# Places of split weights by the order of products, a last group's sums and a head's rotation moved from GpSimd to VectorE, and two spreadings sharing a pair of banks, in a fp32 hybrid layer step on one Trainium2 core

## The chip, the cores and the metric

The kernel runs on one core of a Trainium2 chip (trn2). The metric is the device time of one execution in microseconds; the median of three runs of the kernel before is 2238.82 us (2236.67 to 2243.57). A core has a matrix engine (TensorE, PE in the profile; PEld is its loading of weights), VectorE (DVE), ScalarE (ACT), GpSimd (POOL), SyncE (SP), whose queue issues most of the DMAs here, an on-chip memory of 128 partitions (SBUF), and accumulator banks of 128 partitions by 2 KB (PSUM), into which matmuls write.

## What is computed

One step of a layer: 1024 prompt frames and 64 sample frames, D_MODEL 1024, all in float32.

```python
xn = RMSNorm(x); q, k, v, gates, ... = split(xn @ w_in)
A = retention(q, k, v)          # 4 heads of 256, chunks of 64, rotary on q and k
B = sliding_window_attention()  # 16 heads of 64, 2 K/V heads
x += (sigmoid(ga) * A + sigmoid(gb) * B) @ w_mix_out
x += CrossAttn(RMSNorm(x), memory)
x += SwiGLU(RMSNorm(x))         # w_gate, w_up: 1024 -> 2816, w_down back
y = RMSNorm(x)
```

with, for the rotary part, `concat([x1 * cos - x2 * sin, x2 * cos + x1 * sin])`. The outputs are y for both streams, the retention states and the attention caches.

## The kernel before

**Precision.** Each float32 operand is split into two parts, `hi` (a cast by ScalarE, line 123) and `lo` (the rest, a subtraction by VectorE, line 124), and each product is three matmuls: weight hi by x hi (L209), weight hi by x lo (L210), weight lo by x hi (L212). Frames stand along the free dimension: T = 1088, in two halves of HALF = 544, each of two spans of HC = 272 columns. So nearly every matmul of the kernel is 128 rows by 128 columns of weights by 272 columns of x.

**Strassen.** Dense layers run as 2 x 2 block products by Strassen's scheme: seven products (`strassen`, L250) instead of eight. x stands as operands B11, B21, B22 and the combinations T1 to T4; the combinations of the weights are made anew for each group by `weight_ops` (L171): four sums and differences by GpSimd in the buffers `raw` (L187, L188, L190, L193), and a split of each result into a buffer named `wq` by `put`. The weights are *made* in the order P1, P2, P7, P6, P5, P3, P4, and the products *run* in the order P1, P2, P6, P5, P7, P3, P4. There are two buffers `raw` for the two loaded weight pieces of a group, so the next group's pieces load when the last split of this one is done. A product accumulates in a pair of PSUM banks (`bank_pair`, name `pq`); in the FFN there are four pairs. VectorE adds products and running sums (u1, u2, u3, u5; L256), and `emit` consumes the results.

`new_op` (L144) gives the buffer of a split weight: five places in a ring; once a phase late in the projections has made room, a sixth place, which is given to every sixth weight made. The first group of a phase goes without Strassen (`plain`, L229), since its operand combinations aren't there yet: eight products of half the depth.

**What sets the order.** The code is run through a scheduler that simulates a timeline and decides the order of the instructions on each engine, from priorities, data and free buffers. On the chip each engine takes its own queue in that order, and a semaphore holds it up where what it needs isn't there. `issue_after(x)` orders later instructions behind x in the schedule. `later` is a list of functions that are called at a point inside the next product (`run_later`).

**The four places that matter here.**

1. *First head.* The phase begins with the keys, values and queries of head 0; `rotated` (L600) takes two halves a and b of 128 rows: four VectorE products with cos and sin (L610 to L613), then a -= sb and b += sa on GpSimd (L614, L615), then stores of a and b to DRAM (`d_qkv`). They come back as `ks`, `qs`, are split, and the retention starts with `pss` (scores, L153). The same function rotates the other heads later, when the retention of an earlier head is under way; the products of a coming head then fill TensorE's gaps between the steps of the retention's chain (scores `pss`, output `po`, the spreading of norms `pb`, L843).
2. *The norm ahead of the FFN.* `rstd_f`, the reciprocal root for each frame, is computed as a column of values per block of 128 frames and spread over 128 partitions by matmuls with the identity into a bank, and copied out by ScalarE (`spread`, L327 to L335). Three columns of frames are spread: the last two inside the first FFN group (`plain` of w_gate), by `run_later` ahead of the seventh of its eight block products. In the same stretch the operand combinations T2, T3, T4 are made (VectorE sums `xg`, L1352, ScalarE casts, L123) by `other_sums`.
3. *w_down.* The hidden rows of the FFN are handled in three groups (GROUPS), each with four pairs of output blocks (m = 0, 2, 4, 6). `down.add` (L1514) adds a result to the output tiles y: a product in PSUM by VectorE (L1517), a running sum in SBUF by GpSimd (L1519). y is eight tiles, one of which lies in rstd_f. In the last group (`part=True` in `strassen`), P2 and P4 are left to the finish, which does them by thirds of the columns, so each m has five products.
4. *The last group's tail.* `complete` squares the finished half (L1527, L1530) and sums the squares (L1531) for the final norm.

Of the kernel before, what the change touches and what calls it, by code (L numbers as in the profile page):

```python
# [14 lines left out]
ALU = mybir.AluOpType  # L15
# [94 lines left out]
class Kernel:  # L110
# [32 lines left out]

    def new_op(self):  # L144

        self.turns += self.sixth is not None
        if self.turns and self.turns % 6 == 0:
            return self.sixth.tile([P, 2, 512], F32R, tag="wq", bufs=1, name="wq")
        return self.wp.tile([P, 2, 512], F32R, tag="wq", bufs=5, name="wq")

# [19 lines left out]
    def weight_ops(self, raws, n=512, skip=()):  # L170

        nc = self.nc
        half = [[raws[i][:, j * n:(j + 1) * n] for j in range(2)] for i in range(2)]
        (a11, a12), (a21, a22) = half
        add, sub = ALU.add, ALU.subtract
        w = {}

        def put(name, src):
            if name in skip:
                return  # L180
            q = w[name] = self.new_op()
            self.split(src, q[:, 0, :n], q[:, 1, :n])

        tt = nc.gpsimd.tensor_tensor
        put("P1", a11)
        put("P2", a12)
        tt(out=a11, in0=a11, in1=a21, op=sub)  # L187
        tt(out=a21, in0=a21, in1=a22, op=add)  # L188
        put("P7", a11)
        tt(out=a11, in0=a22, in1=a11, op=sub)  # L190
        put("P6", a11)
        put("P5", a21)
        tt(out=a12, in0=a12, in1=a11, op=sub)  # L193
        put("P3", a12)
        put("P4", a22)
        return w
# [54 lines left out]
    def strassen(self, w, x, emit, part=False):  # L251


        nc = self.nc
        u1, u2, u3, u5 = (self.fp.tile([P, 2, HC], F32, tag=t, bufs=1, name=t) for t in ("u1", "u2", "u3", "u5"))
        add = lambda out, a, b: nc.vector.tensor_tensor(out=out, in0=a, in1=b, op=ALU.add)  # L256
        ps = self.product(w, x, "P1", "B11")
        self.run_later()
        nc.scalar.copy(u1, ps)
        emit(0, 0, None if part else self.product(w, x, "P2", "B21"), u1)  # L260
        add(u2, self.product(w, x, "P6", "T2"), u1)
        add(u5, self.product(w, x, "P5", "T1"), u2)
        ps = self.product(w, x, "P7", "T3")
        add(u3, ps, u2)
        emit(1, 1, ps, u5)
        emit(0, 1, self.product(w, x, "P3", "B22"), u5)
        emit(1, 0, None if part else self.product(w, x, "P4", "T4"), u3)
# [59 lines left out]
    def spread(self, out, r):  # L327
# [7 lines left out]
        nc.scalar.copy(out, pb[:, :n])  # L335

    def run(self):
        nc, tc, io = self.nc, self.tc, self.io
        with ExitStack() as ctx:
# [34 lines left out]
            with ExitStack() as sctx:  # L374
# [3 lines left out]
                self.left = sctx.enter_context(ExitStack())  # L378
                self.sixth, self.turns = None, 0
                self.wp = self.left.enter_context(tc.tile_pool(name="weights", bufs=2, reuse_waits="tile"))  # L380
# [172 lines left out]
    def project_phase(self):  # L553
        nc, tc, io = self.nc, self.tc, self.io
        with ExitStack() as ctx:
# [42 lines left out]
            def rotated(w, h, j):  # L598
# [3 lines left out]
                def emit(i, t, ps, sb):  # L602
# [10 lines left out]
                    tt(out=b, in0=b, in1=cos, op=ALU.mult)  # L613
                    nc.gpsimd.tensor_tensor(out=a, in0=a, in1=sb, op=ALU.subtract)  # L614
                    nc.gpsimd.tensor_tensor(out=b, in0=b, in1=sa, op=ALU.add)  # L615
                    self.store(self.d_qkv[j, 2 * h, :, half(t)], a)
# [50 lines left out]
            for idx, w, act in ((1, "w_ga", AF.Sigmoid), (0, "w_rg", AF.Silu), (2, "w_gb", AF.Sigmoid)):  # L667
                for m in range(0, KT, 2):
                    if (idx, m) == (1, 6):
                        fctx.close()  # L670
                        self.sixth = self.left.enter_context(tc.tile_pool(name="sixth", bufs=1, reuse_waits="tile"))
                        self.sums_pool(ctx)
                        op = ctx.enter_context(tc.tile_pool(name="op", bufs=1, reuse_waits="tile"))
                        mp = ctx.enter_context(tc.tile_pool(name="mp", bufs=1, reuse_waits="tile"))
                        self.dense_psum = lambda: self.norm_psum("pd")
                        memory = self.memory_phase(mp)
# [617 lines left out]
    def cross_out_phase(self):  # L1294
        nc, tc, io = self.nc, self.tc, self.io
        with ExitStack() as ctx:
# [9 lines left out]
            for m, u, (c0, n) in self.m_major(units, CH, tail=2):  # L1306
# [12 lines left out]
                if m == KT - 1:  # L1319
# [5 lines left out]
                    if len(norms) < 3:  # L1325
                        self.later += norms[-1][:3 - len(norms)]
            self.later, self.last_roots = [norms[1][1], norms[2][1]], norms[2][0]

# [41 lines left out]
    def operands_late(self, sums=None):  # L1370
# [6 lines left out]
        if sums is not None:  # L1377
            sums()
            self.other_sums()

    def other_sums(self):
        qs = [self.quarters(k) for k in range(4)]
        for k, (b11, b12, b21, b22) in enumerate(qs):
            self.put_sum("T2", k, b12, b22, b12)
        for k, (b11, b12, b21, b22) in enumerate(qs):
# [19 lines left out]
    def gate_up(self, pairs):  # L1405
# [5 lines left out]
        def roots_then_sums():  # L1411
            self.last_roots()
            with self.tc.issue_after(self.last_step):
                self.other_sums()

# [91 lines left out]
    def down(self, starts):  # L1507
# [5 lines left out]
        half = lambda m, t: y[m][:, t * HALF:(t + 1) * HALF]  # L1513
        def add(m, i, t, ps, sb):  # L1514
            v = half(m + i, t).rearrange("p (b c) -> p b c", b=2)
            if ps is not None:
                nc.vector.tensor_tensor(out=v, in0=ps, in1=v, op=ALU.add)  # L1517
            if sb is not None:
                nc.gpsimd.tensor_tensor(out=v, in0=sb, in1=v, op=ALU.add)  # L1519

# [15 lines left out]
        for gi, g in enumerate(GROUPS):  # L1536
            last = gi == len(GROUPS) - 1
            f0, n = starts[gi], g * P // 2
            for m in range(0, KT, 2):
                def emit(i, t, ps, sb, m=m):  # L1540
                    add(m, i, t, ps, sb)
                    if last and t == 1:
# [218 lines left out]
```

## Time and profile before

| | |
|---|---|
| three runs, median (lowest to highest) | 2238.82 us (2236.67 to 2243.57) |
| the profiled execution's own time | 2245.45 us |
| its span in the trace | 2243.6 us |
| mean granted TensorE clock | 0.988 |
| instructions | 41715 |
| ScalarE busy | 885.9 us (39%) |
| PEld busy | 2107.2 us (94%) |
| DMA packets | 181958, 290.85 MB |

The profile is of one execution. In its rows an instruction is shown as start, duration (both us), engine, line, operation, output <- inputs with buffer numbers left out, shape and count; a bracket at the end gives the idle time of the engine just before and what ended it. A view by windows gives for each stretch the busy time of every engine (with the number of instructions in parentheses), then the granted TensorE clock as a share of full speed, the share of the DMA engines, and GB/s. The page's view in slices gives a digit for each fortieth of the span (56 us).

### The profile page before, as it was taken

The numbers are of one execution on the slowest core, as the hardware profiler recorded it, in microseconds if no ns is written. First come the engines' busy times: TensorE is split into PE (matmuls) and PEld (weight loads), VectorE is DVE, ScalarE is ACT, GpSimd is POOL, SyncE is SP. The second block draws the span as 40 slices with busy tenths as digits, with TensorE's granted clock in tenths as the row PEclk, the third lists the DMA queues.
The fourth block names the chain that finished last, engine by engine and source line by source line (L and its number), as shares of the span: only waits on it lengthen the run. The fifth ranks groups of instructions, "written<-read, shape, count | busy, mean of one in ns | idle before, by whom it ended". The sixth has DMA issues, their size and how long they took to land.

```text
span 2243.6 us, 41715 instructions
## 1 busy us (share of the span) xinstructions
PE 2171.3 (97%) x16435; PEld 2107.2 (94%) x16435; DVE 1592.7 (71%) x2622; ACT 885.9 (39%) x1898; POOL 706.0 (31%) x474
## 2 busy tenths in 40 slices
PE   8899999999999999999999999999999999999986
PEld 8899999999999987779999999999999999999985
DVE  8986878676677668765455565777777777877587
ACT  7333333435434346553233343333223223434333
POOL 1441533342253122220000000015556565434462
PEclk9999999999999999999999999999999999999998
DMA  5433345443544475327343111513342332475323
GB/s 198 160 109 111 118 124 133 136 126 114 166 142 166 157 245 185 108 71 217 118 153 119 39 50 55 164 63 98 117 147 88 103 122 89 164 258 177 93 77 108
DMA packets 181958, 290.85 MB, mean 130 GB/s; under 512 B 40290, under 2 KB 110338, under 8 KB 181762
## 3 DMA queue, kind: packets, MB, share of 16 engines
q1 hardware_dynamic: 177218, 278.74, 39.1%
q10 hardware_dynamic: 4032, 7.80, 0.9%
q8 instruction: 130, 2.13, 0.4%
q0 software_dynamic: 512, 1.64, 0.2%
q14 instruction: 66, 0.54, 0.1%
HBM read 196.95 MB, written 91.16 MB: 128 GB/s over the span
## 4 chain that ended last, share of the span: by engine, by line
PE 72%; DVE 13%; DMA 5%; issue 3%; POOL 3%; ACT 3%; SPq 0%; DVEq 0%; POOLq 0%; ACTq 0%
PE pq L212 13%; PE pq L209 13%; PE pq L210 13%; PE pd L153 7%; PE pd L155 7%; PE pd L154 7%; DVE wq L124 3%; PE pout L1004 1%; DMA hl<-d_op 1%; DVE B L124 1%; PE pss L944 1%; DMA raw<-w_up 1%; DVE T L124 1%; POOL raw L190 1%; ACT wq L123 1%
## 5 line engine op out<-in xcount | busy, mean ns | idle before, releaser
L124 DVE TENSOR_TENSOR wq<-raw,wq 128x512 fp32r<-128x512 f32 (+1 forms) x499 | 461.6, 929 | 152.7 <-ACT wq L123 150.4
L123 ACT CAST wq<-raw 128x512 fp32r<-128x512 f32 (+1 forms) x499 | 303.3, 613 | 560.8 <-PE pq L212 226.5
L209 PE MATMUL pq<-T,wq 128*128 128x272 f32 x1832 | 493.5, 289 | 17.9 <-ACT wq L123 8.7
L210 PE MATMUL pq<-T,wq 128*128 128x272 f32 x1832 | 493.4, 289 | 0.0
L210 PE MATMUL pq<-B,wq 128*128 128x272 f32 x1592 | 430.2, 290 | 7.9 <-DVE B L124 7.9
L209 PE MATMUL pq<-B,wq 128*128 128x272 f32 x1592 | 427.7, 289 | 0.2 <-ACT B L123 0.2
L212 PE MATMUL pq<-T,wq 128*128 128x272 f32 x1832 | 383.2, 290 | 0.0
L209 PEld LDWEIGHTS pq<-T,wq 128*128 128x128 f32 x1832 | 346.4, 189 | 19.9 <-ACT wq L123 9.4
L187 POOL TENSOR_TENSOR raw<-raw 128x512 f32<-128x512 f32 (+1 forms) x59 | 78.2, 1326 | 908.0 <-DVE rs_r L295 483.8
L210 PEld LDWEIGHTS pq<-T,wq 128*128 128x128 f32 x1832 | 346.4, 189 | 0.0
L212 PE MATMUL pq<-B,wq 128*128 128x272 f32 x1592 | 333.9, 290 | 0.0
L210 PEld LDWEIGHTS pq<-B,wq 128*128 128x128 f32 x1592 | 301.1, 189 | 9.8 <-DVE B L124 9.4
L209 PEld LDWEIGHTS pq<-B,wq 128*128 128x128 f32 x1592 | 300.9, 189 | 0.8 <-issue 0.4
L212 PEld LDWEIGHTS pq<-T,wq 128*128 128x128 f32 x1832 | 291.0, 190 | 1.1 <-issue 1.1
L212 PEld LDWEIGHTS pq<-B,wq 128*128 128x128 f32 x1592 | 253.4, 190 | 0.5 <-issue 0.3
L256 DVE TENSOR_TENSOR u<-pq,u 128x544 f32<-128x544 f32 x177 | 127.2, 720 | 88.7 <-PE pq L212 87.7
L190 POOL TENSOR_TENSOR raw<-raw 128x512 f32<-128x512 f32 (+1 forms) x59 | 87.7, 1486 | 131.3 <-DVE wq L124 128.8
L579 DVE TENSOR_TENSOR stage<-pq,u 128x544 f32<-128x544 f32 x112 | 80.4, 718 | 27.1 <-PE pq L212 25.1
L193 POOL TENSOR_TENSOR raw<-raw 128x512 f32<-128x512 f32 (+1 forms) x59 | 86.9, 1474 | 16.6 <-DVE wq L124 13.0
L971 POOL TENSOR_TENSOR t<-t,den 128x768 f32<-128x768 f32 (+2 forms) x34 | 48.9, 1439 | 132.5 <-DVE den L969 33.2
L188 POOL TENSOR_TENSOR raw<-raw 128x512 f32<-128x512 f32 (+1 forms) x59 | 88.5, 1500 | 3.6
L1519 POOL TENSOR_TENSOR y<-u,y 128x544 f32<-128x544 f32 x38 | 64.9, 1711 | 75.3 <-DVE y L1517 58.3
(382 smaller groups left out, 4671.2 us busy)
## 6 DMA issues: line engine op xcount, KB each, us to landing
hl<-d_op SPq DMA_DIRECT2D x85, 272.0 KB, 4.5
d_qkv<-stage SPq DMA_DIRECT2D x44, 272.0 KB, 2.4
d_op<-stage SPq DMA_DIRECT2D x44, 272.0 KB, 2.3
d_op<-ht SPq DMA_DIRECT2D x44, 272.0 KB, 3.3
raw<-w_gate SPq DMA_DIRECT2D x22, 512.0 KB, 3.5
raw<-w_up SPq DMA_DIRECT2D x22, 512.0 KB, 3.7
raw<-w_down SPq DMA_DIRECT2D x16, 512.0 KB, 4.4
d_gate<-stage ACTq DMA_DIRECT2D x28, 272.0 KB, 2.6
```

The source lines that it names most:

```text
L123: self.last_cast = self.nc.scalar.copy(hi, src).ins
L124: return self.nc.vector.tensor_tensor(out=lo, in0=src, in1=hi.bitcast(F32), op=ALU.subtract).ins
L153: mm(ps, wh, xh, start=start, stop=False)
L154: mm(ps, wh, xl, start=False, stop=False)
L155: self.last_mm = mm(ps, wl, xh, start=False, stop=stop).ins
L188: tt(out=a21, in0=a21, in1=a22, op=add)
L190: tt(out=a11, in0=a22, in1=a11, op=sub)
L193: tt(out=a12, in0=a12, in1=a11, op=sub)
L209: mm(ps[:, c, :HC], w[:, 0, ks], x[:, 0, cs], start=start, stop=False)
L210: mm(ps[:, c, :HC], w[:, 0, ks], x[:, 1, cs], start=False, stop=False)
L212: self.last_mm = mm(ps[:, c, :HC], w[:, 1, ks], x[:, 0, c * HC:(c + 1) * HC], start=False, stop=stop).ins
L256: add = lambda out, a, b: nc.vector.tensor_tensor(out=out, in0=a, in1=b, op=ALU.add)
```

## The change

Five edits, in one diff (the names are those above):

- `new_op` no longer gives the sixth place to every sixth weight but to the one for which the sixth place's last holder is used earlier than those of the five (the list `held`), counting uses in the order of products: `put` passes the number of turns by which P7, P6 and P5 run later or earlier than they are made.
- `strassen(part=True)`, of the last group of w_down: the first product is added to y straight from PSUM (VectorE) instead of from its copy u1 (GpSimd).
- `down.add`: in the last group the running sums in SBUF are added by VectorE too.
- `rotated`: for head 0 the last subtraction and addition are VectorE's.
- `spread_both`: the last two spreadings of rstd_f go into the two banks of one pair, with both copies behind them; T3 and T4 (`last_sums`) are issued behind the copies, and only T2 (`second_sums`) ahead.

```diff
-    def new_op(self):
-        self.turns += self.sixth is not None
-        if self.turns and self.turns % 6 == 0:
+    def new_op(self, ahead=0):
+        self.turns += 1
+        turn = self.turns + ahead
+        if self.sixth is not None and self.last_held < min(self.held):
+            self.last_held = turn
             return self.sixth.tile([P, 2, 512], F32R, tag="wq", bufs=1, name="wq")
+        self.held = sorted(self.held)[-4:] + [turn]
         return self.wp.tile([P, 2, 512], F32R, tag="wq", bufs=5, name="wq")
...
-            q = w[name] = self.new_op()
+            q = w[name] = self.new_op({"P7": 2, "P6": -1, "P5": -1}.get(name, 0))
...
         ps = self.product(w, x, "P1", "B11")
         self.run_later()
         nc.scalar.copy(u1, ps)
-        emit(0, 0, None if part else self.product(w, x, "P2", "B21"), u1)
+        if part:
+            emit(0, 0, ps, None)
+        else:
+            emit(0, 0, self.product(w, x, "P2", "B21"), u1)
...
+    def spread_both(self, outs, rs):
+        pb = self.bank_pair()
+        for i, (out, r) in enumerate(zip(outs, rs)):
+            for j, (a, w) in enumerate(self.spans(out.shape[1])):
+                self.last_mm = self.nc.tensor.matmul(pb[:, i, a:a + w], r[:, j:j + 1].broadcast_to([P, P]), self.ident,
+                                                     start=True, stop=True).ins
+        for i, out in enumerate(outs):
+            self.spreaded = self.nc.scalar.copy(out, pb[:, i, :out.shape[1]]).ins
...
-                    nc.gpsimd.tensor_tensor(out=a, in0=a, in1=sb, op=ALU.subtract)
-                    nc.gpsimd.tensor_tensor(out=b, in0=b, in1=sa, op=ALU.add)
+                    tt = tt if h == 0 else nc.gpsimd.tensor_tensor
+                    tt(out=a, in0=a, in1=sb, op=ALU.subtract)
+                    tt(out=b, in0=b, in1=sa, op=ALU.add)
...
-            self.later, self.last_roots = [norms[1][1], norms[2][1]], norms[2][0]
+            self.later = [lambda: self.spread_both([self.rstd_f[:, c0:c0 + n] for c0, n in CH[1:]], rs[1:]), self.last_sums]
+            self.last_roots = norms[2][0]
...
+    def second_sums(self):
+        for k in range(4):
+            _, b12, _, b22 = self.quarters(k)
+            self.put_sum("T2", k, b12, b22, b12)
+
+    def last_sums(self):
+        with self.tc.issue_after(self.spreaded):
             self.other_sums()
...
-                self.other_sums()
+                self.second_sums()
...
-        def add(m, i, t, ps, sb):
+        def add(m, i, t, ps, sb, by=nc.gpsimd):
...
-                nc.gpsimd.tensor_tensor(out=v, in0=sb, in1=v, op=ALU.add)
+                by.tensor_tensor(out=v, in0=sb, in1=v, op=ALU.add)
...
-                    add(m, i, t, ps, sb)
+                    add(m, i, t, ps, sb, nc.vector if last else nc.gpsimd)
```

How it moves instructions, at three places. Line numbers of the changed kernel are higher by 3 (up to the Strassen part, L259 there is L256 here) to 27 (L1546 is L1519).

GpSimd's queue in the last group of w_down, from the middle of m = 2 on, before (L187, L188, L190 and L193 make weights, L1519 adds a running sum u to an output tile):

```order
L187 TENSOR_TENSOR raw<-raw 128x384
L188 TENSOR_TENSOR raw<-raw 128x384
L1519 TENSOR_TENSOR y_22080<-u_24319,y_22080 128x544
L1519 TENSOR_TENSOR y_22080<-u_24320,y_22080 128x544
L190 TENSOR_TENSOR raw<-raw 128x384
L1519 TENSOR_TENSOR y_22079<-u_24320,y_22079 128x544
L193 TENSOR_TENSOR raw<-raw 128x384
L1519 TENSOR_TENSOR y_22080<-u_24455,y_22080 128x544
L187 TENSOR_TENSOR raw<-raw 128x384
L188 TENSOR_TENSOR raw<-raw 128x384
```

and a part near the end of its queue after the change (L190, L191, L193 and L196 are the same four):

```order
L1546 TENSOR_TENSOR y_22082<-u_23882,y_22082 128x544
L190 TENSOR_TENSOR raw<-raw 128x384
L191 TENSOR_TENSOR raw<-raw 128x384
L193 TENSOR_TENSOR raw<-raw 128x384
L196 TENSOR_TENSOR raw<-raw 128x384
L190 TENSOR_TENSOR raw<-raw 128x384
L191 TENSOR_TENSOR raw<-raw 128x384
```

No addition stands between the weight sums any more. They stand on VectorE now; there, during m = 2, after the change (L259 are the running sums, L1544 adds of a product from PSUM, L1546 of a running sum, L1558 the sum of squares, L124 splits):

```order
L259 TENSOR_TENSOR u_24318<-pq,u_24317 128x544
L1544 TENSOR_TENSOR y_22079<-pq,y_22079 128x544
L124 TENSOR_TENSOR wq<-raw,wq 128x384
L1546 TENSOR_TENSOR y_22079<-u_24318,y_22079 128x544
L124 TENSOR_TENSOR wq<-raw,wq 128x384
L1544 TENSOR_TENSOR y_22078<-pq,y_22078 128x544
L1546 TENSOR_TENSOR y_22079<-u_24319,y_22079 128x544
L124 TENSOR_TENSOR wq<-raw,wq 128x384
L1546 TENSOR_TENSOR y_22078<-u_24319,y_22078 128x544
L1544 TENSOR_TENSOR y_22079<-pq,y_22079 128x544
L1558 TENSOR_TENSOR rstd<-rstd,sq 128x544
```

Three of the eleven are moved there, between splits that the next products need.

ScalarE's queue around the spreading of rstd_f, before (T tiles are the split combinations T2, two k each in T_16827 and T_16828, and T3 in T_16829 and T_16830; L335 copies a spreading out of its bank):

```order
L123 CAST T_16827<-xg_15873 128x544 x2
L123 CAST T_16828<-xg_15874 128x544 x2
L123 CAST T_16829<-xg_15873 128x544 x2
L123 CAST T_16830<-xg_15874 128x544
L123 CAST wq<-raw 128x512
L335 COPY rstd_f<-pb 128x384
L123 CAST T_16830<-xg_15874 128x544
L335 COPY rstd_f<-pb 128x320
```

and after:

```order
L123 CAST T_16827<-xg_15873 128x544 x2
L123 CAST T_16828<-xg_15874 128x544 x2
L123 CAST wq<-raw 128x512
L351 COPY rstd_f<-pq 128x384
L351 COPY rstd_f<-pq 128x320
L123 CAST T_16829<-xg_15873 128x544 x2
L123 CAST T_16830<-xg_15874 128x544 x2
```

The casts of T3 moved from before the copies to behind both of them. The matmuls of the two spreadings stand at the same place of TensorE's queue both times.

VectorE's queue in the first head, around the end of the keys' rotation, before (L610 to L613 products with cos and sin, L460 sums of squares of the first norm, L579 and L256 read products from PSUM):

```order
L579 TENSOR_TENSOR stage_553<-pq,u_562 128x544
L612 TENSOR_TENSOR stage_552<-stage_552,rope 128x544
L124 TENSOR_TENSOR wq<-raw,wq 128x512
L460 TENSOR_TENSOR rstd<-rstd,xsq 128x544
L611 TENSOR_TENSOR stage_553<-stage_553,rope 128x544
L124 TENSOR_TENSOR wq<-raw,wq 128x512
L460 TENSOR_TENSOR rstd<-rstd,xsq 128x544 x2
L613 TENSOR_TENSOR stage_553<-stage_553,rope 128x544
L124 TENSOR_TENSOR wq<-raw,wq 128x512
L460 TENSOR_TENSOR rstd<-rstd,xsq 128x544
L256 TENSOR_TENSOR u_855<-pq,u_854 128x544
```

and after (the same lines are L595, L626 to L629, L476 and L259; L631 and L632 are the moved subtraction and addition):

```order
L628 TENSOR_TENSOR stage_552<-stage_552,rope 128x544
L632 TENSOR_TENSOR stage_552<-stage_552 128x544
L124 TENSOR_TENSOR wq<-raw,wq 128x512
L476 TENSOR_TENSOR rstd<-rstd,xsq 128x544
L627 TENSOR_TENSOR stage_553<-stage_553,rope 128x544
L631 TENSOR_TENSOR stage_552<-stage_552,stage_553 128x544
L124 TENSOR_TENSOR wq<-raw,wq 128x512
L476 TENSOR_TENSOR rstd<-rstd,xsq 128x544 x2
L629 TENSOR_TENSOR stage_553<-stage_553,rope 128x544
L631 TENSOR_TENSOR stage_552<-stage_552,stage_553 128x544
L124 TENSOR_TENSOR wq<-raw,wq 128x512
L476 TENSOR_TENSOR rstd<-rstd,xsq 128x544
```

Three of the four moved instructions of the keys stand ahead of the sum L259 that follows next, the fourth behind it.

Over the whole program the counts stay (TensorE the same, VectorE 24 more, GpSimd 24 fewer) but for two more activation-table loads on ScalarE. TensorE's order is the same up to the first head's queries, is chosen anew by the scheduler in the retention that follows (75 more matmuls of projections stand ahead of the first `pss`: 753 against 678), and is the same again from the gate projections to the FFN's last group.

More of the change, by code (lines that the diff above doesn't have):

```diff
@@ L378, in run @@
                 self.left = sctx.enter_context(ExitStack())
-                self.sixth, self.turns = None, 0
+                self.sixth, self.turns, self.held, self.last_held = None, 0, [], 0
                 self.wp = self.left.enter_context(tc.tile_pool(name="weights", bufs=2, reuse_waits="tile"))
@@ L671, in project_phase @@
                         self.sixth = self.left.enter_context(tc.tile_pool(name="sixth", bufs=1, reuse_waits="tile"))
+                        self.last_held = self.turns
                         self.sums_pool(ctx)
@@ L1378, in operands_late @@
             sums()
+            self.second_sums()
+            self.other_sums()
+    def second_sums(self):
[4 more added lines that the diff above has]
+        with self.tc.issue_after(self.spreaded):
             self.other_sums()
@@ L1382, in other_sums @@
         qs = [self.quarters(k) for k in range(4)]
-        for k, (b11, b12, b21, b22) in enumerate(qs):
-            self.put_sum("T2", k, b12, b22, b12)
         for k, (b11, b12, b21, b22) in enumerate(qs):
@@ L1413, in roots_then_sums @@
             with self.tc.issue_after(self.last_step):
-                self.other_sums()
+                self.second_sums()
         r = [self.rstd_f[:, t * HALF:(t + 1) * HALF].rearrange("p (b c) -> p b c", b=2) for t in range(2)]
```

## The prediction

> **What bounds the kernel now.** I read the page's totals and slices first, then the view by windows, then TensorE's own idle rows.
>
> ```profile
> span 2243.6 us, 41715 instructions
> PE 2171.3 (97%) x16435; PEld 2107.2 (94%) x16435; DVE 1592.7 (71%) x2622; ACT 885.9 (39%) x1898; POOL 706.0 (31%) x474
> PE   8899999999999999999999999999999999999986
> PEclk9999999999999999999999999999999999999998
> 57.00:120.00 63.00, 53.87 (x407) 53.13 (x406) 59.96 (x98) 22.18 (x40) 31.98 (x20) 0.95 0.43 140
> 120.00:480.00 360.00, 352.01 (x2799) 343.35 (x2798) 272.08 (x478) 139.52 (x310) 131.44 (x89) 1.00 0.43 125
> 1500.00:1535.00 35.00, 32.43 (x237) 31.95 (x235) 31.00 (x44) 15.74 (x26) 10.46 (x7) 0.90 0.13 38
> 1535.00:1950.00 415.00, 415.00 (x3337) 415.00 (x3336) 314.73 (x362) 123.22 (x207) 242.62 (x160) 1.00 0.35 113
> 2142.00:2206.00 64.00, 52.00 (x380) 50.53 (x378) 50.76 (x55) 20.93 (x37) 41.18 (x30) 0.95 0.26 76
> ```
>
> TensorE is the bound: 97% of the span, and 415.00 of 415.00 us in the long middle of the FFN. There is no arithmetic to save here, since the change leaves TensorE's instructions as they are. All that can be won is TensorE's idle time and the time at a lower clock, and these lie where the change is: the first head (57 to 120), the norm of the FFN (1500 to 1535) and the last group (2142 to 2206). There VectorE is at 95%, 89% and 79%, so it is also the engine on which added work costs.
>
> TensorE's idle rows in these places (the bracket is the wait):
>
> ```profile
> 80.17 0.39 PE L209 MATMUL pq<-T,wq 128*128 128x272 f32 x1 [3.64 <-DVE u L256]
> 114.37 0.39 PE L153 MATMUL pss<-qs,ks 128*128 128x256 f32 x1 [3.91 <-ACT qs L123]
> 1511.05 1.51 PE L334 MATMUL pb<-ident,rs_r 128*128 128x128 f32 x6 [2.06 <-ACT rstd_f L335]
> 1513.07 0.59 PE L209 MATMUL pq<-b,wq 128*128 128x272 f32 x1 [0.52 <-ACT rstd_f L335]
> 2159.72 0.59 PE L209 MATMUL pq<-T,wq 128*128 128x272 f32 x1 [2.44 <-ACT wq L123]
> 2175.66 0.39 PE L209 MATMUL pq<-T,wq 128*128 128x272 f32 x1 [2.90 <-ACT wq L123]
> 2192.08 0.39 PE L209 MATMUL pq<-T,wq 128*128 128x272 f32 x1 [3.39 <-ACT wq L123]
> ```
>
> Idle time has a second price, which the windows of 3.4 us behind two of these gaps show (the seventh figure is the granted clock):
>
> ```profile
> 81.00:84.40 3.40, 3.40 (x17) 3.40 (x16) 3.40 (x6) 1.49 (x3) 0.98 (x1) 0.51 0.87 313
> 115.20:118.60 3.40, 3.40 (x19) 3.40 (x18) 3.36 (x7) 0.16 (x1) 1.01 (x1) 0.50 0.00 0
> 118.60:122.00 3.40, 3.40 (x29) 3.40 (x29) 2.97 (x5) 2.64 (x5) 2.36 (x2) 1.00 0.51 154
> 1514.60:1518.10 3.50, 3.50 (x17) 3.50 (x17) 3.50 (x6) 1.13 (x2) 0.00 (x0) 0.51 0.00 0
> 2159.70:2163.20 3.50, 3.48 (x15) 3.48 (x16) 2.05 (x2) 2.31 (x5) 3.50 (x4) 0.51 0.39 112
> 2176.80:2180.20 3.40, 3.40 (x18) 3.40 (x17) 3.09 (x3) 0.95 (x2) 3.37 (x3) 0.50 0.30 102
> 2190.50:2193.90 3.40, 1.82 (x14) 1.82 (x15) 2.66 (x3) 2.60 (x5) 3.40 (x3) 1.00 0.00 0
> ```
>
> 17 matmuls in place of 29 are 12/29 of 3.4 us, 1.4 us lost per such window.
>
> **Head 0's rotation.** Eight GpSimd instructions go (two halves, keys and queries, two adds each), eight go to VectorE.
>
> ```profile
> L615 POOL TENSOR_TENSOR stage<-stage 128x544 f32<-128x544 f32 x4 | 7.3, 1819 | 3.9 <-DVE stage L610 2.0 <-DVE stage L613 1.9
> L614 POOL TENSOR_TENSOR stage<-stage,stage 128x544 f32<-128x544 f32 x4 | 7.1, 1784 | 5.1 <-DVE stage L611 2.6 <-DVE stage L612 2.6
> 77.63 1.84 DVE L460 TENSOR_TENSOR rstd<-rstd,xsq 128x544 f32<-128x544 f32 x1
> 80.63 0.71 DVE L460 TENSOR_TENSOR rstd<-rstd,xsq 128x544 f32<-128x544 f32 x1
> 81.27 0.71 DVE L579 TENSOR_TENSOR stage<-pq,u 128x544 f32<-128x544 f32 x1
> ```
>
> One add takes GpSimd 1.8 us, and while it runs an add of VectorE on the same memory takes 1.84 instead of 0.71 (80.63 to 81.27: one each 0.64). So each of the four keys' adds costs VectorE 0.64 and gives back about 1.1. Ahead of the sum u that ends the wait at 80.17 stand three of them: 4 x 1.1 - 3 x 0.64 = 2.5 us sooner, and of 3.64 some 1.1 stay, too little for the slow window (-1.4). The queries' adds end, by VectorE's order, some 3.8 us sooner than GpSimd's last, after five more adds and two more splits in its queue; through store and load these reach `pss`, whose wait is 3.91. Besides, 75 more matmuls stand ahead of `pss`, and at 0.124 us each (3337 in 415.00) they are 9 us that would cover the rest. At most 2.5 + 1.4 + 3.9 + 1.2 = 9.0. At least 3.8, if VectorE's queue alone decides and the 75 wait for it too. I take **-7.5**, nearer the upper end because of the fill.
>
> **The other heads.** The scheduler set TensorE's order in 120 to 480 anew. There 352.01 of 360 us are busy:
>
> ```profile
> PE pb L843 <- ACT ret_o L839: 5.6, 5, 1.5
> ```
>
> The norm of a block (L843) is what TensorE waits for most, 5.6 us in five waits. The new order can end them or repeat them: 0, from -4 to +4; the fill between the steps of the chain counts 48 to 98 matmuls (6 to 12 us) before, 51 to 103 after.
>
> **Places of the split weights.** Until the sixth place exists nothing changes, and in the FFN's middle there is no idle time to win (415.00 of 415.00). A weight that got its place too late would show there; its queue of five or six places is as long as before. 0, from -1 to +1. The two more activation tables lie on ScalarE, at 39%: 0, to +1.
>
> **The spreadings.** The second waits for a bank until the first's copy is out (2.06), and the next product until the second's (0.52):
>
> ```profile
> 1509.45 0.65 ACT L123 CAST T<-xg 128x544 fp32r<-128x544 f32 x1 [1.26 <-DVE xg L1352]
> 1510.00 0.61 ACT L123 CAST wq<-raw 128x512 fp32r<-128x512 f32 x1
> 1510.52 0.47 ACT L335 COPY rstd_f<-pb 128x384 f32<-128x384 f32 x1
> 1512.60 0.43 ACT L335 COPY rstd_f<-pb 128x320 f32<-128x320 f32 x1 [0.59 <-PE pb L334]
> ```
>
> The first copy stood behind a cast of T3 that VectorE's sum held up. The first spreading's matmuls ended at 1511.05 - 2.06 = 1509.0. With one pair for both, the second's follow at once (half of 1.51, since they ran at half clock) and end by 1509.8; with T3 behind them the two copies, 0.47 and 0.43, are out by 1510.8. So TensorE goes on at 1510.8, not 1513.07: 2.3 us sooner. With 1 us idle the slow clock goes too, 1.4 us in the quoted window and some 0.8 between 1513.07 and its start. I take **-4.5**, from -2.3 (the clock drops still) to -5.
>
> The Trainium skill ("TensorE: Matmul & The Clock Gate", section "What's actually happening") says that the clock halves after at least one idle window of about 3.4 us that runs free of the kernel. By that a wait shorter than a window costs no clock, the slow windows are owed to something else and stay, and the sum below would be -14 instead of -19. The rows speak against it: 0.51 stands behind a wait of 2.44 (2159.72), and 1.00 behind the longer one of 3.39 (2192.08), which lies across two windows.
>
> **The last group.** TensorE waits three times for the cast of a weight that GpSimd's sum held up, and that sum stands behind additions to y:
>
> ```profile
> L1519 POOL TENSOR_TENSOR y<-u,y 128x544 f32<-128x544 f32 x13 | 21.1, 1631 | 10.3 <-DVE u L256 8.5 <-DVE y L1517 1.8
> 2170.65 2.98 POOL L1519 TENSOR_TENSOR y<-u,y 128x544 f32<-128x544 f32 x2 [1.29 <-DVE u L256]
> 2173.59 1.47 POOL L190 TENSOR_TENSOR raw<-raw 128x384 f32<-128x384 f32 x1
> 2175.10 0.51 ACT L123 CAST wq<-raw 128x384 fp32r<-128x384 f32 x1 [0.28 <-POOL raw L190]
> 2152.53 0.56 DVE L124 TENSOR_TENSOR wq<-raw,wq 128x384 fp32r<-128x384 f32 x1 [2.08 <-ACT wq L123]
> L124 DVE TENSOR_TENSOR wq<-raw,wq 128x384 fp32r<-128x384 f32 x16 | 19.0, 1200 | 6.3 <-ACT wq L123 6.2
> ```
>
> At 2170.65 GpSimd first waits for a running sum, then adds twice, 2.98 us, and only then makes the weight whose cast releases TensorE at 2175.66. These additions leave GpSimd; L190 then waits for the split ahead of it alone. The three waits are 8.7 us, and behind two of them lies a slow window, 2.8: at most -11.5. What is late next is VectorE. It gets 16 x 0.64 = 10.2 us, and gets back what GpSimd's additions cost it: 16 splits at 1.20 instead of 0.56 are 10.2 us, the adds of squares and operands a few more, some 15 in all, of which the additions caused the share of their 21.1 us in GpSimd's 41.18, and of two more like them, so 9. Its 50.8 us of 64 become about 52, against 47 us of TensorE's 380 matmuls at 0.124. So the stretch can't end up under 52; with VectorE at the share it has in 57 to 120, 95%, it takes 55 to 57, and I take **-7**, from -3 to -11.5. An addition that waits for its product now holds up the splits behind it on VectorE, as it held up GpSimd's sums; that is the reason for the lower end.
>
> **Sum.** -7.5 - 4.5 - 7 = -19 against the profiled execution's 2245.45: 2226.5. That execution was 6.6 us above the median of 2238.82; from the median it is 2219.8, and I predict **2220**.
>
> **Rivals.**
> - *VectorE takes the place of GpSimd.* In both stretches its queue decides: -3.8 and -3, the spreading -2.3: -9, **2230**. For it: 95% in 57 to 120, four moved adds between splits. Against it: the contention given back is about as large as the added work. 0.16.
> - *The slow clock stays.* The idle time goes, but the half-clock windows, of which head 0 has two, the spreading one and a half and the last group two (5 x 1.4, of which my terms count some 5), come from elsewhere: -14, **2225**. For it: 2192.08 had the longest wait of the last group and no slow window. Against it: each slow window quoted stands right behind a wait of 2 us or more. 0.06.
> - *The fill runs out (slower).* The 75 matmuls ahead of the first `pss` are missing later, and the chain's links wait for ScalarE as at L843. There are 16 links (four heads of four blocks). If each lost the 1.5 us of the longest such wait, +24, and each second a slow window, 8 x 1.4 = +11, then with -19 it is +16, **2255**. It decides from (19 + 6.7) / 16 = 1.6 us a link. Against it: the fill per link counts the same, and only five waits were there before. 0.04.
> - *The change does half.* The last group's weights wait for their loads (GpSimd idles 10.4 us there for `raw`), and the first head stays as it is: -4.5 and a little, with +4 from the other heads about 0 to -5, **2236**. The rows with ACT as releaser speak against it, since the loads end before the additions begin. 0.08.
>
> ```profile
> L187 POOL TENSOR_TENSOR raw<-raw 128x384 f32<-128x384 f32 x3 | 3.0, 1015 | 10.4 <-DMA raw<-w_down 10.4
> ```
>
> **Numbers.** The forecast has 0.66, with all three terms near their upper ends inside it (-9 - 5 - 11.5 - 4: 2209). Measurement tells about 0.3%, 6.7 us, from no change, so "same" is 2232.1 to 2245.5: the third rival and a small part of the first, 0.10. Slower 0.04, faster 0.86. The range takes in 2209 and the first two thirds of the third rival: 2208 to 2235.
>
> **What would show it.** In the changed kernel: no wait over 1.5 us ahead of `pss`, and the granted clock 1.00 in 80 to 120; the two copies of rstd_f next to each other and TensorE's next product within 1.2 us of the last spreading; no GpSimd addition after 2142, no wait over 1 us for `wq`, and VectorE over 90% there. It is wrong if VectorE's splits follow additions that wait for TensorE, if TensorE waits for L843 more than 12 us in all in the retention, or if idle time shows up in the FFN's middle.

## The result, and the profile after

The changed kernel takes 2227.36 us (median of six runs, 2223.84 to 2228.64), the kernel before 2240.82 in six runs of its own (2236.67 to 2247.76). The ratio is 0.9936, 95% interval 0.9918 to 0.9954: about 14 us faster. The two profiled executions differ by more, 2245.45 to 2227.08 us, since that of before was 4.6 us above its median; what is placed in the program below is placed by these two. Each trace is of one execution: in the stretch from 697 to 1508 us, where of all edits only the rule for the places acts, the three other traces with the old rule (`no_places`, `only_last`, `only_rot` below) lose 2.0 us and win 1.6 and 2.7 against that of before. So a difference of 2 us in one stretch of one trace can be chance.

The page's totals, slices and windows of the changed kernel (the windows are set where the same work lies now):

```profile
span 2225.0 us, 41705 instructions
PE 2165.0 (97%) x16435; PEld 2101.6 (94%) x16435; DVE 1574.7 (71%) x2646; ACT 886.0 (40%) x1900; POOL 665.3 (30%) x450
PE   9989998999999999999999999999999999999996
57.00:120.00 63.00, 60.26 (x468) 59.44 (x467) 61.73 (x110) 23.96 (x42) 20.55 (x13) 0.97 0.43 137
120.00:480.00 360.00, 344.29 (x2717) 334.89 (x2715) 264.22 (x468) 135.79 (x302) 136.85 (x88) 0.99 0.42 123
1490.00:1525.00 35.00, 34.10 (x276) 33.91 (x275) 33.58 (x50) 16.79 (x31) 13.63 (x8) 1.00 0.02 6
1525.00:1940.00 415.00, 415.00 (x3338) 415.00 (x3336) 307.72 (x365) 120.68 (x203) 234.93 (x160) 1.00 0.35 113
2132.00:2192.00 60.00, 57.59 (x441) 56.47 (x439) 55.31 (x82) 25.28 (x46) 20.38 (x15) 0.97 0.29 87
```

The three places have filled up: 60.26 us of TensorE against 53.87 in the first head, a clock of 1.00 against 0.90 at the spreadings, 57.59 us of 60 in the last group. But 120 to 480, for which no edit is meant, has lost: 344.29 against 352.01. TensorE's five longest groups of waits from 57 to 480 in the changed kernel, by engine and line waited for (total, times, longest):

```profile
PE pkv L156 <- DVE vb L772: 7.2, 1, 7.2
PE pb L861 <- ACT ret_o L857: 2.6, 3, 1.2
PE po L158 <- DVE ss L124: 2.3, 2, 1.7
PE pq L212 <- DVE stage L595: 2.3, 1, 2.3
PE pss L156 <- DVE kt L763: 2.1, 2, 1.3
```

The fourth is the wait at 115 us, still in the first head. One wait of 7.2 us was not there before. The timelines of VectorE and SyncE show what is behind it, and the view of DMA issues (each with its size and the median from issue to landing) what the transfers took:

```profile
369.77 0.72 DVE L595 TENSOR_TENSOR stage<-pq,u 128x544 f32<-128x544 f32 x1 [9.17 <-DMA d_qkv<-stage]
354.57 0.67 SPq L120 DMA_DIRECT2D d_rb<-rb  x1
355.35 4.87 SPq L120 DMA_DIRECT2D d_qkv<-stage  x2
360.31 4.25 SPq L117 DMA_DIRECT2D raw<-w_v  x1
364.65 2.33 SPq L117 DMA_DIRECT2D vf<-d_qkv  x1
d_rb<-rb SPq DMA_DIRECT2D x1, 1024.0 KB, 14.4
d_qkv<-stage SPq DMA_DIRECT2D x2, 272.0 KB, 12.7
```

The store of the bias table d_rb (1 MB, a row of 1 KB 64 times for each of 16 heads) is under way for 14.4 us. Two stores of finished stage tiles stand right behind it in SyncE's new order and take 12.7 us. VectorE's next addition wants one of these tiles, waits 9.17 us, and everything behind it in its queue waits too, the `vb` of the retention among it. Before, in the old order, the next stage store came 11 us after d_rb was issued:

```profile
352.70 0.67 SPq L120 DMA_DIRECT2D d_rb<-rb  x1
364.02 0.34 SPq L120 DMA_DIRECT2D d_qkv<-stage  x1
```

The time of the same numbered matmul in both traces, before minus after, tells where the rest went: 0.6 us were won when the first head's last products begin (76), 6.1 at 176, 7.8 at 337, 0.6 at 385. At the start of the gate projections (634) 4.0 us were *lost*, at their end (697) 1.6. At the spreadings 4.8 us were won, from 2129 to the end 13.0. (Between 76 and 634 the order of the matmuls differs, so the numbers in between are near, not exact.)

### The profile page after: what moved, and what is told of

Same layout as the page of the kernel before. It is cut to its first block, busy times and chain, and to the rows that moved or that the text cites. A ratio compares the mean times of both kernels' runs of the same rounds, so it can differ in the third digit from the quotient of the medians.

```text
span 2225.0 us, 41705 instructions
## 1 busy us (share of the span) xinstructions
PE 2165.0 (97%) x16435; PEld 2101.6 (94%) x16435; DVE 1574.7 (71%) x2646; ACT 886.0 (40%) x1900; POOL 665.3 (30%) x450
## 4 chain that ended last, share of the span: by engine, by line
PE 75%; DVE 13%; DMA 5%; ACT 3%; issue 3%; POOL 1%; SPq 0%; DVEq 0%; ACTq 0%; POOLq 0%
PE pq L215 14%; PE pq L212 14%; PE pq L213 14%; PE pd L156 8%; PE pd L158 8%; PE pd L157 8%; DVE wq L124 2%; PE pout L1022 1%; DMA hl<-d_op 1%; PE pss L962 1%; DVE B L124 1%; DVE stage L595 1%; DVE T L124 1%; DMA d_qkv<-stage 1%; PE pp L1001 1%
## 5 line engine op out<-in xcount | busy, mean ns | idle before, releaser
L124 DVE TENSOR_TENSOR wq<-raw,wq 128x512 fp32r<-128x512 f32 (+1 forms) x499 | 443.9, 893 | 147.3 <-ACT wq L123 144.8
L190 POOL TENSOR_TENSOR raw<-raw 128x512 f32<-128x512 f32 (+1 forms) x59 | 79.5, 1347 | 971.4 <-DVE rs_r L301 482.4
L259 DVE TENSOR_TENSOR u<-pq,u 128x544 f32<-128x544 f32 x177 | 127.3, 719 | 81.1 <-PE pq L215 80.5
L193 POOL TENSOR_TENSOR raw<-raw 128x512 f32<-128x512 f32 (+1 forms) x59 | 83.3, 1412 | 119.2 <-DVE wq L124 102.0
L595 DVE TENSOR_TENSOR stage<-pq,u 128x544 f32<-128x544 f32 x112 | 80.3, 717 | 38.2 <-PE pq L215 20.7
L191 POOL TENSOR_TENSOR raw<-raw 128x512 f32<-128x512 f32 (+1 forms) x59 | 89.7, 1520 | 3.5
L196 POOL TENSOR_TENSOR raw<-raw 128x512 f32<-128x512 f32 (+1 forms) x59 | 82.7, 1401 | 4.5
L1464 POOL TENSOR_TENSOR stage<-stage,rstd_f 128x544 f32<-128x544 f32 x40 | 63.9, 1607 | 39.1 <-ACT stage L1463 39.1
```

The costliest lines, as they stand in the source:

```text
L124: return self.nc.vector.tensor_tensor(out=lo, in0=src, in1=hi.bitcast(F32), op=ALU.subtract).ins
L595: nc.vector.tensor_tensor(out=o, in0=ps, in1=sb, op=ALU.add)
```

## The experiments

Each kernel has runs of the kernel before beside it; its ratio to them has an interval of about plus or minus 0.2% (4 us), so differences of 2 us between two experiments are not told apart by the times alone. Where the difference of two medians and that of two ratios are not the same, both are given.

### Leaving out one part

**The rotation.** Undone:

```diff
-                    tt = tt if h == 0 else nc.gpsimd.tensor_tensor
+                    tt = nc.gpsimd.tensor_tensor
```

> The rotation of head 0 is GpSimd's again, all else as in the changed kernel. TensorE's order in the retention is then that of before. Theory (the first head gained about 6 us by index of the matmuls and the retention that follows gave it back, 7.2 us of it in one wait for vb): the time is that of the changed kernel, 2227, within 3 us. Rival (the forecast's term: head 0 is worth 7.5 us by itself): 2233 to 2236.

Measured: 2221.57 us (2219.75 to 2223.77), ratio 0.9904 (0.9884 to 0.9924). It is not the same as the changed kernel but 5.8 us *faster*: that edit costs more than it brings. By the traces, at 634 us the changed kernel is 4.0 us behind the kernel before and this one 0.8 ahead. TensorE's order in the retention is again that of before and the wait for vb is gone. Theory and rival both missed, on the same side: they took the loss to be at most what the first head gains.

**The last group's sums.** `emit` as before, and GpSimd for the sums:

```diff
-                    add(m, i, t, ps, sb, nc.vector if last else nc.gpsimd)
+                    add(m, i, t, ps, sb)
```

> The last group's sums are GpSimd's again and the first product is added from its copy, all else as in the changed kernel. The forecast's term: 7 us more than the changed kernel, 2234. Theory from the two traces (13 us between the last group's start and the end): 13 us more, 2240, with the three waits of 2.4 to 3.4 us for wq back.

Measured: 2233.22 us (2227.03 to 2236.25), ratio 0.9954 (0.9937 to 0.9971), 5.9 us slower than the changed kernel by the medians, 4 by the ratios, whose intervals overlap. That is near the forecast's 7, and far from the theory's 13. By the trace, 6.1 of the 13 us from 2129 on were still won without this edit. The three waits of 2.4 to 3.4 us for a weight's cast, which the theory wanted back, did not come back: they are 0.7 us in all, and one wait of 3.2 for VectorE's part of a split stands instead.

```profile
PE pq L215 <- DVE wq L124: 3.4, 2, 3.2
PE pq L212 <- ACT wq L123: 0.7, 1, 0.7
```

Something else in the change helps the last group.

**The spreadings.** Two pairs of banks again:

```diff
-            self.later = [lambda: self.spread_both(...), self.last_sums]
-            self.last_roots = norms[2][0]
+            self.later, self.last_roots = [norms[1][1], norms[2][1]], norms[2][0]
...
                 self.second_sums()
+                self.other_sums()
```

> The two spreadings have a pair of banks each again, with T3 and T4 ahead, all else as in the changed kernel. Forecast and trace agree: 4.5 to 4.8 us more, 2232, with the waits of 2.06 and 0.5 us and the half clock behind them back. Rival (the slow clock has another cause): 2.3 us more, 2229.5, and the half clock seen in both.

Measured: 2229.51 us (2226.85 to 2234.42), ratio 0.9940 (0.9922 to 0.9957), 2.1 us slower by the medians, 0.9 by the ratios. In its trace both waits are back:

```profile
1509.21 0.93 PE L340 MATMUL pb<-ident,rs_r 128*128 128x128 f32 x6 [2.05 <-ACT rstd_f L341]
1510.65 0.51 PE L212 MATMUL pq<-b,wq 128*128 128x272 f32 x1 [0.52 <-ACT rstd_f L341]
```

Here the second spreading took 0.93 us instead of 1.51, since it was over before the half clock began at 1510.8, and only one window of 3.4 us was slow, not two. Of the 4.8 us by the trace, 3.5 are lost without the edit. The time is that of the rival, 2229.5, but the half clock is seen in this kernel alone; the times can't tell 2.3 from 4.8.

**The places.** Every sixth weight in the sixth place again:

```diff
-        self.turns += 1
-        turn = self.turns + ahead
-        if self.sixth is not None and self.last_held < min(self.held):
-            self.last_held = turn
+        self.turns += self.sixth is not None
+        if self.turns and self.turns % 6 == 0:
```

> Every sixth weight gets the sixth place again, all else as in the changed kernel. Forecast: the same time, 2227 within 1 to 2 us, and TensorE as busy in the middle of the FFN. Rival (places hold up splits in the down groups or the end): 3 us more or less, seen between 1950 and the end.

Measured: 2229.81 us (2228.51 to 2230.38), ratio 0.9940 (0.9922 to 0.9957), 2.5 us slower by the medians, 0.9 by the ratios: not told from nothing. Its trace tells more. In the gate projections (634 to 697) the changed kernel wins 2.4 us, this one 0.2. From 2129 on it wins 9.0 us, not 13.0. That is 6 us in its disfavour; 3.0 of them are hidden in the time because in this execution less was lost ahead of the gate projections. At the end the wait that opens the last group is back, beside shorter ones for weights (first this kernel, 2120 to 2210, then the changed one):

```profile
PE pq L209 <- ACT wq L123: 4.2, 3, 1.6
PE pq L209 <- DVE y L1540: 2.5, 1, 2.5
```

```profile
PE pq L212 <- ACT wq L123: 1.5, 2, 0.8
PE pq L212 <- DVE y L1544: 0.4, 1, 0.4
```

The cast of the first weight of m = 2, by ScalarE's timeline in this kernel and in the changed one:

```profile
2145.27 0.52 ACT L123 CAST wq<-raw 128x384 fp32r<-128x384 f32 x1 [7.93 <-DMA raw<-w_down]
```

```profile
2138.76 0.51 ACT L123 CAST wq<-raw 128x384 fp32r<-128x384 f32 x1 [3.52 <-DMA raw<-w_down]
```

It comes 6.5 us earlier in the changed kernel, though that one runs the same numbered matmul ahead of it 0.8 us later: 7.3 us earlier by the work. The first load of m = 2 is issued at 2135.54 against 2142.10; a load waits until the weights of m = 0 that were made in its buffer are split. With the new rule the scheduler sets these splits one by one between the splits of operands; with the old one, three of them stand together at the end (2139.85 to 2142.49), behind the addition that ends the wait of 2.5 us.

### One part alone

**The new places, on the kernel before.**

> The kernel before with the new rule for the sixth place and nothing else. Theory from the traces (2.4 us in the gate projections, where two waits for weights go, and some 4 to 6 in the last group, where P6 got the place of the P7 before it): 6 to 8 us less than before, 2233 to 2235. Forecast: 0 within 1, 2240.

Measured: 2234.23 us (2231.67 to 2238.18), ratio 0.9967 (0.9955 to 0.9978), 7.4 us by the ratio. The theory holds, and the forecast's zero does not. By matmuls, 2.7 us are won in the gate projections and 6.3 from 2129 to the end. GpSimd still makes the additions of the last group here, and yet TensorE's waits for the cast of a weight are 0.7 us from 2120 to 2210, not 8.7 (first the kernel before, then this one):

```profile
PE pq L209 <- ACT wq L123: 8.7, 3, 3.4
```

```profile
PE pq L212 <- ACT wq L123: 0.7, 1, 0.7
```

**The last group's sums, on the kernel before** (the two edits to `emit` and `add`).

> The kernel before with the last group's sums on VectorE and the first product added from PSUM, and nothing else. Forecast: 7 us less, 2235. Theory from the traces without the new places (9.0 us between the last group's start and the end): 9 us less, 2233. Rival (VectorE takes GpSimd's place): 3 us less.

Measured: 2233.96 us (2231.68 to 2238.02), ratio 0.9963 (0.9951 to 0.9976): 8.3 us by the ratio, and 9.2 by the matmuls from 2129 on. Forecast and theory are both within the interval; the rival is not. TensorE's waits for a cast are 2.6 us here. So the old places and GpSimd's additions were both needed for the 8.7 us of waits, and what the two edits win there overlaps: 6.3 and 9.2 us alone, 13.0 together.

**The rotation of head 0 on VectorE, on the kernel before.**

> The kernel before with the rotation of head 0 on VectorE and nothing else. Theory: what the first head gains the collision with the store of d_rb takes back and more, 4 to 6 us more than before, 2245 to 2247. Forecast: 7.5 us less, 2233.

Measured: 2244.46 us (2240.79 to 2251.98), ratio 1.0011 (1.0000 to 1.0022). Not faster in any case. The loss of 4 to 6 us that was expected is not shown: the interval reaches from nothing to 5 us. By its trace, 7.7 us are won at 176, and at 634 it is 1.7 us behind.

### What the rotation runs into

**The store of d_rb from another queue.** It is issued by ScalarE:

```diff
-        self.store(self.d_rb.rearrange("h (i c) -> h i c", c=256), rb...)
+        nc.scalar.dma_start(self.d_rb.rearrange("h (i c) -> h i c", c=256), rb...)
```

> The changed kernel with one edit: the 1 MB store of the bias table (d_rb) is issued from ScalarE's queue instead of SyncE's, where two stores of stage tiles and two weight loads stand behind it. The order of TensorE is the same. Theory (that store holds up the stage tiles, so VectorE waits 9 us and TensorE 7.2 us): 6 to 7 us less than the changed kernel, 2220 to 2221.5, without the wait for vb near 365. Rival (the DMA engines are full of that store whatever queue it is issued from): 2227 and the wait stays. Second rival (the retention's order is worse by itself): the wait goes, but not more than 3 us are won, since they are lost at the waits behind it.

Measured: 2228.16 us (2224.04 to 2230.68), ratio 0.9935 (0.9922 to 0.9949): nothing won. The wait stays, and the stage stores take as long on SyncE's queue beside it as they took behind it:

```profile
PE pkv L156 <- DVE vb L772: 6.9, 1, 6.9
d_rb<-rb ACTq DMA_DIRECT2D x1, 1024.0 KB, 14.2
d_qkv<-stage SPq DMA_DIRECT2D x2, 272.0 KB, 12.3
```

The order on SyncE's queue is not the cause; the time and the wait are those of the first rival.

**The same without the rotation.**

> The same edit on the kernel whose rotation of head 0 is GpSimd's again, where the loads and stores behind the store of d_rb did not hold up TensorE for more than 1.6 us. Theory: 0 to 2 us less than that kernel's 2221.6, so 2219.5 to 2221.6, and the two kernels with the edit within 2 us of each other. Rival (head 0's rotation on VectorE is worth 6 us once the collision is gone): 6 us more than the kernel with both.

Measured: 2223.23 us (2218.06 to 2227.09), ratio 0.9914 (0.9898 to 0.9929), not told apart from the 0.9904 without the queue edit. "Within 2 us of each other" failed with the run before: 2228.16 against 2223.23.

**The table at another time.** In `project_phase`, after the last head:

```diff
-                    if h == 1:
+                    if h == 3:
                         self.bias_table()
```

> The changed kernel with the bias table, and so its store of 1 MB (d_rb), made after the last head instead of after the second. TensorE's order is the same up to the place of the table, and new from there to the end of the retention. Issuing the store from another queue did not help, so the theory is now that the DMA engines themselves are full of its packets, and that only another time for it helps: the wait of 7 us for vb near 365 goes and the time is 5 to 7 us less than the changed kernel, 2220 to 2222. Rival (the retention's order after the rotation on VectorE is worse by itself): the wait goes, and other waits of the retention take at least half of it, 2224 to 2228.

Measured: 2222.33 us (2221.05 to 2222.87), ratio 0.9906 (0.9890 to 0.9921), 5.0 us faster than the changed kernel. Up to the table's old place (matmul 2450, at 329 us) the two traces stay within 1 us; by 384 this one is 10.5 us ahead, of which 5.5 are left at the end of the gate projections. The wait for vb is gone. Of the 5 us that are lost again, 3.9 lie between 558 and 610, around the table's new place, whose store is issued at 574.70; the longest single wait is there now, at 592.82:

```profile
PE pq L212 <- ACT u L262: 2.5, 1, 2.5
```

The time is at the edge of the theory's 2220 to 2222; that other stretches take half of what is won is what the rival said. The run does not decide between them.

**The same without the rotation.**

> The same with the rotation of head 0 on GpSimd. Theory: with the table out of the way the first head's 6 us are VectorE's gain, so this kernel is slower than the one before by 4 to 6 us or, if the new order still loses some of it, by 0 to 3. Rival (the rotation on VectorE is worth nothing in any order): this one is faster by 2 us or more.

Measured: 2230.42 us (2229.92 to 2232.01), ratio 0.9945 (0.9933 to 0.9958): 8.1 us slower than with the rotation on VectorE: the theory's sign, but beyond its 4 to 6, and as much as the first head gives at its best (at matmul 1200 the traces with the rotation on VectorE are 5.1 to 8.0 us ahead of the kernel before, 6.1 in the changed kernel). By the trace, moving the table cost this kernel 7.9 us up to 697 against the one with the table in its place, where the longest group of waits grew from 5.6 to 9.5 us:

```profile
PE pb L861 <- ACT ret_o L857: 9.5, 7, 2.6
```

So the orders of the retention that were run differ by several microseconds either way, also where the edit was meant for something else.

**The table after the third head** (`h == 2`).

> The changed kernel with the bias table made after the third head. In SyncE's queue its store (d_rb) then stands, as in the changed kernel, ahead of two stores of stage tiles (d_skv), a load of vf and two weight loads (w_ga). Theory (the stores and loads right behind that store are what costs, whichever head it is): a wait of 5 us or more for a stage tile or an operand comes back, at the place of the store, and the time is 2225 to 2228. Rival (the wait of the changed kernel came of that one place in the retention's order): no such wait, 2220 to 2223.

Measured: 2217.05 us (2214.73 to 2218.83), ratio 0.9884 (0.9865 to 0.9904), the fastest of all, 26 us below the kernel before and 10 below the changed one. The theory fell and the rival held: the store stands ahead of stage stores here as well and no such wait comes.

```profile
462.90 0.67 SPq L120 DMA_DIRECT2D d_rb<-rb  x1
466.84 0.35 SPq L120 DMA_DIRECT2D d_skv<-stage  x1
471.51 3.40 SPq L120 DMA_DIRECT2D d_skv<-stage  x1
d_skv<-stage SPq DMA_DIRECT2D x3, 272.0 KB, 7.1
```

Two stores were issued 4 and 9 us behind it, not at once; 7.1 us is the median of these and one issued just ahead of it. VectorE waited for none of them. By these traces, what costs is not the order itself but a tile that is wanted again within the 14 us that the store lasts.

## Why the prediction was right, and where it was not

The forecast was faster, 2220 in a range of 2208 to 2235; it is 2227.36, and about 14 us of the 19 forecast came. By its own steps:

- **Bound.** Right. TensorE's busy share stays at 97%, and all that was won is its idle time and its slow clock.
- **The spreadings, -4.5.** The mechanism was right, the size is near the upper end of what was shown: 4.8 by the trace, but the times of the kernel without it show only 2.1 with some 4 of uncertainty. The other four traces without this edit (without the spreadings, and each of the three edits alone) have the same waits of 2.05 and 0.52, and are 1.3 to 2.8 us faster here than the profiled execution before, which had two slow windows where they have one or none, and a second spreading of 1.51 us where theirs takes 0.93. Against them the edit wins 2.0 to 3.5. As forecast, both copies stand side by side and TensorE goes on soon, at the granted clock of 1.00:

```profile
1507.73 1.06 PE L348 MATMUL pq<-ident,rs_r 128*128 128x128 f32 x8
1509.68 0.39 PE L212 MATMUL pq<-b,wq 128*128 128x272 f32 x1 [0.90 <-ACT rstd_f L351]
```

  The waits fell from 2.06 and 0.52 us to 0.90, by 1.7, and the time by 4.8. Most of the rest is the slow clock, which went with the idle time: no trace with this edit has a slow window here, and four of the five without it have one or two. So the rival in which it stays fell here.
- **The last group, -7.** The size is near: alone it brings 8.3 us, left out it costs 5.9 (4 by the ratios). The mechanism was right in part. The waits for weights go when the additions leave GpSimd, but they also go when the additions stay and only the places change; the forecast read them as the additions' alone. VectorE is at 55.31 of 60 us, 92%, as forecast, and it did not become the bound; the longest wait for a weight is 0.8 us. One slow window stayed, at 2163.8 (granted clock 0.50 up to 2167.2). What GpSimd's sums had cost VectorE came back: a split of 384 columns takes 734 ns on average, against 1200.

```profile
L124 DVE TENSOR_TENSOR wq<-raw,wq 128x384 fp32r<-128x384 f32 x16 | 11.6, 734 | 3.3 <-ACT wq L123 3.3
```

- **The places, 0 within 1.** Wrong; alone they bring 7.4 us (by the ratio's interval 4.9 to 10.1). The step argued that there was no idle time to win in the middle of the FFN, where TensorE is still at 415.00 of 415.00. It did not ask for the same in the gate projections, where TensorE waited 1.46 us at 670 and 0.88 us at 684 (0.17 in all in the changed kernel), nor in the last group. There each m makes five weights, not seven, and by the code the ring of six gave P6 the place of the P7 before it in three of four m, with only two products between the use of the one and that of the other; the new rule gave P6 that place in two. Shown is that this edit sets the last group's splits and loads earlier; which of the changed places does it was not tried.
- **Head 0, -7.5, and the other heads, 0 from -4 to +4.** The first is near, the second wrong. 6.1 us are won at matmul 1200. The wait of 3.6 us for u became 0.5, and the 3.9 us ahead of `pss` became one of 2.3 a little before it, with a slow window behind. So two signs that the forecast named did not come, no wait over 1.5 us there and a clock of 1.00 up to 120:

```profile
115.07 0.36 PE L212 MATMUL pq<-B,wq 128*128 128x272 f32 x1 [2.28 <-DVE stage L595]
115.80:119.20 3.40, 3.40 (x19) 3.40 (x18) 3.40 (x6) 1.13 (x2) 1.08 (x2) 0.50 0.02 2
```

  (The Trainium skill, "TensorE: Matmul & The Clock Gate", section "What's actually happening", asks for an idle window of about 3.4 us ahead of the half clock; this run shows it behind a wait of 2.28 us.) Then the retention, set anew, gave back 10.1 us by 634, beyond the bound of +4; 7.3 of them are lost between 337 and 385, where the wait for vb lies. That bound was read from the waits of TensorE before; the step left out what the new order does to SyncE's queue and the buffers that its stores release. What was missing is a look at every queue of the new order: the rows for d_rb and the stage tiles stood in it. The rival "the fill runs out" was not what came: TensorE's waits at L861 fell from 5.6 to 2.6 us in 57 to 480.
- **The sum.** Between the two profiled executions the 19 us came, but not as they were added up: 6.1 won in the first head, 10.1 lost behind it, 2.4 won in the gate projections, 2.5 from there to the spreadings (no edit is shown to be the cause), 4.8 at the spreadings, 0.3 behind them and 13.0 in the last group, where the new places have a share. By the medians it is 14. Two terms were wrong with opposite signs, the places by some 7 us and the retention by some 10, so that the whole came out near is partly luck.

How much of the rotation's cost is the store of d_rb, and how much the new order otherwise, is only partly settled: with the table moved, the rotation on VectorE is in the fastest kernel of all, but the kernel without the rotation and with the table after the third head was not run, and without the rotation, moving the table behind the last head cost 8 us, for a cause that is open.

## What to carry to other kernels

Where an edit makes a scheduler set a long stretch anew, ask for each queue what stands right behind its longest transfers, not only for the engine that bounds: here 7 of the 8 us that had been won were lost where a tile was wanted again beside a store of 14 us. When a buffer's place is chosen by a rule, follow the rule through each kind of group, and look for idle time at the borders, not in the middle. An edit that wins in its place and loses elsewhere is found by leaving it out: without the rotation the same change is 0.9904 instead of 0.9936, and with the table after the third head 0.9884. Before a size is read from one trace, look at the same place in the traces of other kernels that are the same there: the spreadings' 4.8 us were 2.0 to 3.5 against four of them.

## What the runs showed of the hardware

A store of 1 MB made of rows of 1 KB, read from 16 partitions, took 13.0 to 14.5 us in every order (72 to 81 GB/s by these numbers). The two stores of 272 KB next on SyncE's queue took 12.7 us with it on the same queue and 12.3 with it on another (medians). On the page of the kernel before, their median is 2.4:

```profile
d_qkv<-stage SPq DMA_DIRECT2D x44, 272.0 KB, 2.4
```
